# A decoder layer's gated MLP: the up product with the hi and lo parts of the activations side by side

## The chip, the cores and the metric

One core of one Trainium2 chip runs the whole program. The metric is the device time of one execution in microseconds, as the median of several executions.

## The reference

One layer of a decoder on 256 tokens of width 1024, in float32. The change lies in the second half, the gated MLP with a causal convolution of width 3, which is all that is quoted here:

```python
x = x + merged.astype(x.dtype) @ w_out[i]
x = x + conv_ffn(rmsnorm(x, norm_ffn[i]), w_up[i], conv_w[i], conv_b[i], w_down[i])
return rmsnorm(x, norm_final)

def rmsnorm(x, g):
    y = xf * lax.rsqrt(jnp.mean(xf * xf, axis=-1, keepdims=True) + RMS_EPS)
    return y * g

def conv_ffn(x, w_up, conv_w, conv_b, w_down):
    h = x @ w_up                        # (256, 1024) @ (1024, 5632)
    h = depthwise_causal_conv3(h, conv_w) + conv_b
    a, u = jnp.split(h, 2, axis=-1)     # 2816 columns each
    return (jax.nn.silu(a) * u) @ w_down
```

## The kernel before

**Numbers in two parts.** Each float32 operand of a product is split into a rounded part, hi, and the rest, lo, both of type fp32r. A product is three matmuls: lo times hi, hi times lo, hi times hi. The helper `mm3` (L238) issues them, at L239, L240 and L241, so nearly all of TensorE's rows carry one of these three lines. In `mm3` the second argument pair is the stationary side (loaded by LDWEIGHTS), the third the moving side.

**Weights.** They come from memory in units of 128 x 2048 elements (class `Unit`): one DMA on SP's queue into `raw` (L218), then in two halves of 1024 columns ScalarE copies the hi part (L223, `whi`) and VectorE subtracts for the lo part (L227, `wlo`). Five buffers of each kind rotate. The MLP uses per step i (0 to 10) the units `fa{i}`, `fu{i}` (up weights of the a and u columns) and `fd{i}` (down weights).

**The up product.** Tokens are on the moving side: `h_hi` and `h_lo` (tiles `hn_hi`, `hn_lo`) hold the activations transposed, 8 tiles of 128 rows (k) by 256 tokens, times the norm's weight but not yet divided by the norm's root. For each chunk ch of 128 columns (22 of a, 22 of u), `up` (L891) makes 8 times `mm3`, so 24 matmuls of 256 columns, into one of four PSUM tiles `g`. `by_rstd` (L792, L795) then multiplies by the row factor `rows` on VectorE, into one of three quarters of tile `xn1`; this also frees the PSUM tile.

**The rest of a chunk.** `conv` is one ScalarE activation (L879) and two VectorE operations (L881) in tile `cy`; SiLU of a is on ScalarE (L899), the gate product on VectorE (L901, `sa`), then the split into `fh` (ScalarE, L904) and `fl` (VectorE, L905). `later` (L702) queues the down product of the chunk: 12 matmuls of 512 columns into the four sums `acc`, issued one chunk later (three later for the last three chunks). The first of these 12 has `fl` on its stationary side, so TensorE waits there if `fl` is late.

**The way into the MLP.** Up to L867 the order on the engines is written by hand: the residual add, squares, the transposes of x into the four `acc` banks (`turned`, list `xT`), the split into `h_hi`, `h_lo` (`turn_hi` L786 on ScalarE, `turn_lo` L789 on VectorE), the products of chunk 0 and 1 of both sides (`firsts`), and `rows` (L851). From L869 on the order within each engine is the scheduler's; each engine runs its list strictly in that order.

Of the kernel before, what the change touches and what calls it, by code (L numbers as in the profile page):

```python
# [10 lines left out]
F32 = mybir.dt.float32  # L11
F32R = mybir.dt.float32r
# [3 lines left out]

P = 128
WARM = 16
S = 256
D = 1024  # L20
KC = D // P
# [106 lines left out]
def decoder_layer(ctx: ExitStack, tc, x, small_b, table, w1, wts, norms, out):  # L128
# [112 lines left out]
        nc.tensor.matmul(ps, ah, bh, start=False, stop=stop)  # L241

    mix = ctx.enter_context(tc.tile_pool(name="mix", bufs=1))
    o_hi = mix.tile([P, KC, S], F32R, name="o_hi")
    o_lo = mix.tile([P, KC, S], F32R, name="o_lo")
    mixer = ctx.enter_context(ExitStack())
    qkv = mixer.enter_context(tc.tile_pool(name="qkv", bufs=1))
    att = mixer.enter_context(tc.tile_pool(name="att", bufs=1))
# [433 lines left out]
    turn = [0]  # L682

    def gtile():
        turn[0] ^= 1
        return pools[turn[0]].tile([P, 512], F32, name="g")[:, :S]

    late = ctx.enter_context(tc.tile_pool(name="late", bufs=1))

# [73 lines left out]
    h_hi, h_lo = normed_tiles()  # L763
    spare = [act_pool.tile([P, D], F32, name=f"xn{t}") for t in range(NT)]
    rows, scaled = spare[1][:, 0:S], [spare[1][:, i * S:(i + 1) * S] for i in range(1, 4)]
    HALF = [slice(n * 512, (n + 1) * 512) for n in range(2)]

    def add(t, n):
# [23 lines left out]
    def by_rstd(ps):  # L792
        u = scaled.pop(0)
        scaled.append(u)
        nc.vector.tensor_mul(u, ps, rows)  # L795
        return u

    fu = dict(first)
    firsts = [gtile() for _ in range(4)]
# [9 lines left out]
    with tc.manual_schedule(engines={mybir.EngineType.Activation, mybir.EngineType.DVE, mybir.EngineType.Pool,  # L809
                                     mybir.EngineType.PE}):  # L810

        sq = {}
        for t in range(NT):
            flush(t, 0)
            add(t, 0)
            sq[t, 0] = square(t, 0)
        flush(0, 1)
        add(0, 1)
        xT += turned(0)
        flush(1, 1)  # L820

        def split_x(c0):

            for c in (c0, c0 + 1):
                turn_hi(c)
            for c in (c0, c0 + 1):
                turn_lo(c)
        split_x(0)
        add(1, 1)
        split_x(2)  # L830
        for t in range(NT):
            sq[t, 1] = square(t, 1)
        first_products(0, h_hi, range(4))

        rs = [rstd_of([sq[t, 0], sq[t, 1]], f"f{t}") for t in range(NT)]
        xT += turned(1)
        first_products(0, h_lo, range(4))
        split_x(4)
        split_x(6)
        for i in range(2):  # L840
            u_f.lo(i, 2)
        u_n = Unit("fa1")
        fu["fa1"] = u_n.views
        for i in range(2):
            u_n.hi(i, 2)
        first_products(0, h_hi, range(4, KC))

        rp = psa.tile([P, 512], F32, name="acc00")[:, :S]
        for t in range(NT):
            nc.tensor.matmul(rp[:, t * P:(t + 1) * P], rs[t].to_broadcast([P, P]), ident, start=True, stop=True)  # L850
        on_act = [nc.scalar.activation(rows, rp, AF.Copy)]  # L851
        for i in range(2):
            u_n.lo(i, 2)
        first_products(0, h_lo, range(4, KC))
        u_n = Unit("fu1")
        fu["fu1"] = u_n.views
        for i in range(2):
            u_n.hi(i, 2)
        for i in range(4):
            for k in range(KC):  # L860
                u = fu[("fa0", "fu0")[i % 2]]
                nc.tensor.matmul(firsts[i], u[1][:, k, i // 2 * P:(i // 2 + 1) * P], h_hi[:, k, :], start=False,  # L862
                                 stop=k == KC - 1)
            if i < 3:
                firsts[i] = by_rstd(firsts[i])
            if i < 2:
                on_dve = u_n.lo(i, 2)  # L867
    waiting.clear()
    with tc.issue_after(on_act[0].ins), tc.issue_after(on_dve.ins):  # L869
        fu["fd0"] = unit("fd0")  # L870


    merge.close()
# [11 lines left out]
    for i in range(NFF // 2):  # L885
        with tc.issue_after(on_act[3 + i].ins) if i in (1, 2) else ExitStack():
            ua, uu, ud = [fu.pop(f"f{w}{i}", None) or unit(f"f{w}{i}") for w in "aud"]
        for c in range(2):
            ch = 2 * i + c

            def up(u):  # L891
                ps = gtile()
                for k in range(KC):
                    mm3(ps, u[0][:, k, c * P:(c + 1) * P], u[1][:, k, c * P:(c + 1) * P],
                        h_hi[:, k, :], h_lo[:, k, :], k == 0, k == KC - 1)
                return by_rstd(ps)
            a = conv(firsts[2 * ch] if ch < 2 else up(ua), ch)
            sa = mpool.tile([P, S], F32, name="sa")
            nc.scalar.activation(sa, a, AF.Silu)  # L899
            b = conv(firsts[1] if ch == 0 else by_rstd(firsts[3]) if ch == 1 else up(uu), NFF + ch)  # L900
            nc.vector.tensor_mul(sa, sa, b)  # L901
            fh = mpool.tile([P, S], F32R, name="fh", bufs=4)
            fl = mpool.tile([P, S], F32R, name="fl", bufs=4)
            nc.scalar.activation(fh, sa, AF.Copy)  # L904
            nc.vector.tensor_sub(fl, sa, fh.bitcast(F32))  # L905
            later(acc, fh, fl, ud, c, ch == 0, ch == NFF - 1, 1 if ch < NFF - 3 else 3)
# [39 lines left out]
```

## Time and profile before

| | us |
|---|---|
| median of three executions | 432.51 |
| the three | 432.37, 432.51, 433.72 |
| the profiled execution | 432.46 |
| its span, first to last instruction | 430.7 |
| TensorE busy in the span | 420.8 |
| VectorE busy | 307.1 |
| ScalarE busy | 240.0 |

The span starts at the first instruction and all stamps count from there. Busy matmuls overlap in the profile, so their pace is read from the distance of their starts, not from their durations. A group "x4" is a run of four operations with their joint duration.

### The profile page before, as it was taken

Reading aid. Unit: us, or ns where it says so; the run is one execution under the profiler, and the core shown is the slowest. Engines: PE = TensorE matmul, PEld = TensorE weight load, DVE = VectorE, ACT = ScalarE, POOL = GpSimd, SP = SyncE. Lnnn points to the kernel's source line nnn. Section 1 sums busy time; section 2 is a strip of 40 time slices with the busy share of each in tenths; the row PEclk is TensorE's granted clock in tenths of the full one; section 3 lists DMA queues with packets and bytes.
Section 4 is the critical chain, followed back from the end, with each engine's and each line's share of the span. In section 5 each row is a group of like instructions: output and inputs, shape, how many; then the busy total and the mean of one; then the engine's idle time right before and its main releaser. Section 6 shows DMA issues by size and latency. Waiting matters only on the chain.

```text
span 430.7 us, 7724 instructions
## 1 busy us (share of the span) xinstructions
PE 420.8 (98%) x3104; PEld 388.3 (90%) x3104; DVE 307.1 (71%) x637; ACT 240.0 (56%) x421; POOL 12.9 (3%) x19
## 2 busy tenths in 40 slices
PE   8999999999999999999999999999999999999993
PEld 8998888887789998999998999999999999999982
DVE  4756753798874697539255899888697797786854
ACT  6443282448777774454346868457465465574423
POOL 3301000000000000000000000000000000000001
PEclk9999999999999999999999999999999999999998
DMA  8989619431209784554530367673462652700002
GB/s 299 397 321 326 238 68 367 177 130 75 99 5 339 288 327 168 196 189 158 189 151 0 139 253 257 231 269 135 183 256 81 251 203 95 290 0 2 2 0 97
DMA packets 12611, 78.09 MB, mean 181 GB/s; under 512 B 1392, under 2 KB 1408, under 8 KB 4640
## 3 DMA queue, kind: packets, MB, share of 16 engines
q1 hardware_dynamic: 12000, 75.48, 46.8%
q0 software_dynamic: 576, 2.12, 1.5%
q8 instruction: 24, 0.39, 0.4%
q14 instruction: 11, 0.09, 0.1%
HBM read 76.52 MB, written 1.07 MB: 180 GB/s over the span
## 4 chain that ended last, share of the span: by engine, by line
PE 90%; ACT 3%; issue 2%; DMA 2%; DVE 1%; POOL 1%; POOLq 0%; SPq 0%; ACTq 0%
PE g L239 21%; PE g L241 20%; PE g L240 20%; PE acc L239 6%; PE acc L240 6%; PE acc L241 6%; PE o L488 2%; PE t L469 2%; PE g L806 2%; DMA raw<-in_wts_dram 2%; PE s L455 1%; PE g L862 1%; PE o L555 1%; ACT tt L506 1%; POOL wlo L227 1%
## 5 line engine op out<-in xcount | busy, mean ns | idle before, releaser
L227 DVE TENSOR_TENSOR wlo<-raw,whi 128x1024 fp32r<-128x1024 f32 (+2 forms) x130 | 152.7, 1205 | 47.6 <-ACT whi L223 47.3
L239 PE MATMUL g<-hn_hi,wlo 128*128 128x256 f32 x632 | 180.4, 285 | 0.1
L240 PE MATMUL g<-hn_lo,whi 128*128 128x256 f32 x632 | 180.0, 285 | 0.0
L241 PE MATMUL g<-hn_hi,whi 128*128 128x256 f32 x632 | 179.7, 284 | 0.0
L223 ACT ACTIVATE whi<-raw 128x1024 fp32r<-128x1024 f32 (+2 forms) x130 | 129.2, 1038 | 37.7 <-PE g L241 30.6
L239 PEld LDWEIGHTS g<-hn_hi,wlo 128*128 128x128 f32 x632 | 121.1, 192 | 3.4 <-issue 1.4
L240 PEld LDWEIGHTS g<-hn_lo,whi 128*128 128x128 f32 x632 | 121.1, 192 | 1.2 <-issue 0.5
L241 PEld LDWEIGHTS g<-hn_hi,whi 128*128 128x128 f32 x632 | 121.2, 192 | 1.0 <-issue 1.0
L881 DVE SCALAR_TENSOR_TENSOR cy<-xn,small_b,cy 128x255 f32<-128x255 f32 (+1 forms) x88 | 41.7, 481 | 10.8 <-ACT cy L879 9.8
L879 ACT ACTIVATE cy<-xn,small_b 128x256 f32<-128x256 f32 x44 | 26.1, 594 | 17.2 <-DVE xn L795 17.2
L239 PE MATMUL acc<-whi,fl 128*128 128x512 f32 x88 | 34.6, 393 | 0.0
L240 PE MATMUL acc<-wlo,fh 128*128 128x512 f32 x88 | 34.4, 391 | 0.0
L241 PE MATMUL acc<-whi,fh 128*128 128x512 f32 x88 | 34.2, 389 | 0.0
L904 ACT ACTIVATE fh<-sa 128x256 fp32r<-128x256 f32 x22 | 9.1, 414 | 33.1 <-DVE sa L901 33.1
L795 DVE TENSOR_TENSOR xn<-g,xn 128x256 f32<-128x256 f32 x44 | 18.5, 421 | 9.6 <-PE g L241 9.0
L673 ACT ACTIVATE gl<-g 128x256 f32<-128x256 f32 x24 | 9.1, 378 | 21.7 <-PE g L241 21.7
L241 PEld LDWEIGHTS acc<-whi,fh 128*128 128x128 f32 x88 | 16.5, 188 | 3.6
L239 PEld LDWEIGHTS acc<-whi,fl 128*128 128x128 f32 x88 | 16.6, 188 | 3.1
L240 PEld LDWEIGHTS acc<-wlo,fh 128*128 128x128 f32 x88 | 16.6, 189 | 2.8
L239 PE MATMUL g<-o_hi,wlo 128*128 128x256 f32 x64 | 18.2, 286 | 0.0
L240 PE MATMUL g<-o_lo,whi 128*128 128x256 f32 x64 | 18.1, 283 | 0.0
L241 PE MATMUL g<-o_hi,whi 128*128 128x256 f32 x64 | 17.9, 283 | 0.0
(180 smaller groups left out, 495.6 us busy)
## 6 DMA issues: line engine op xcount, KB each, us to landing
raw<-in_wts_dram SPq DMA_DIRECT2D x62, 1024.0 KB, 4.9
gl<-in_w_dram SPq DMA_DIRECT2D x8, 512.0 KB, 7.4
raw<-in_wts_dram SPq DMA_DIRECT2D x2, 804.0 KB, 7.4
raw<-in_wts_dram SPq DMA_DIRECT2D x3, 512.0 KB, 7.1
T<-tvd POOLq DMA_DIRECT2D x1, 1280.0 KB, 12.9
xs<-in_x_dram SPq DMA_DIRECT2D x2, 516.0 KB, 3.7
out_dram<-raw SPq DMA_DIRECT2D x4, 256.0 KB, 2.2
T<-tvd POOLq DMA_DIRECT2D x1, 768.0 KB, 8.1
```

The lines of the kernel that those rows point to most:

```text
L223: nc.scalar.activation(self.parts[0][:, sl], self.raw[:, sl], AF.Copy)
L227: return (eng or nc.vector).tensor_sub(self.parts[1][:, sl], self.raw[:, sl], self.parts[0][:, sl].bitcast(F32))
L239: nc.tensor.matmul(ps, al, bh, start=start, stop=False)
L240: nc.tensor.matmul(ps, ah, bl, start=False, stop=False)
L241: nc.tensor.matmul(ps, ah, bh, start=False, stop=stop)
L469: nc.tensor.transpose(ps[:, i * P:(i + 1) * P], b, ident)
L488: nc.tensor.matmul(po[64 * h:64 * h + 64, cols], a, b, start=i == 0, stop=i == len(steps) - 1)
L673: nc.scalar.activation(gl[c][:, b, :], chunk_T(plain(u, c)), AF.Copy)
L795: nc.vector.tensor_mul(u, ps, rows)
L879: on_act.append(nc.scalar.activation(y, u, AF.Identity, bias=vec_c[:, 3, ch:ch + 1], scale=vec_c[:, 2, ch:ch + 1]))
L881: nc.vector.scalar_tensor_tensor(y[:, sh:], u[:, :S - sh], vec_c[:, w, ch:ch + 1], y[:, sh:], op0=ALU.mult, op1=ALU.add)
L904: nc.scalar.activation(fh, sa, AF.Copy)
```

## The change

From step i = 3 on (`NORMED = 3`, so 16 chunks of a and 16 of u), the up product reads the activations from one new tile `parts` (`h_parts`), in which for every k the hi and the lo part of the normed activations stand side by side: 512 columns. The two matmuls that have the weights' hi part on the stationary side, times `h_hi` and times `h_lo`, become one of 512 columns over both halves; the one with the weights' lo part stays, 256 columns. So a chunk has 16 matmuls in place of 24. The right half of the PSUM bank holds hi times lo and has to be added: ScalarE copies it to SBUF (tile `xn0`), and VectorE adds it to the left half, where `by_rstd` stood. Since no factor is applied there any more, the activations in `parts` are already divided by the root: `weighted_T` (ScalarE, 8 operations of 128 x 256) writes x times the norm's weight into two tiles `gl`, and `norm_parts`, called twice when i = 2, multiplies by `rows` (VectorE, 128 x 1024), copies the hi part (ScalarE, 128 x 1024) and subtracts for the lo part (VectorE, 128 x 1024). Chunks 0 to 5 keep the old way, with `h_hi`, `h_lo` and `by_rstd`. `o_hi` and `o_lo` of the attention part become halves of one tile of the same name `parts`, whose place is used again here.

```diff
+NORMED = 3
-    o_hi = mix.tile([P, KC, S], F32R, name="o_hi")
-    o_lo = mix.tile([P, KC, S], F32R, name="o_lo")
+    o_parts = mix.tile([P, KC, 2, S], F32R, name="parts")
+    o_hi, o_lo = o_parts[:, :, 0, :], o_parts[:, :, 1, :]
...
+    copies = [spare[0][:, i * S:(i + 1) * S] for i in range(4)]
...
+    h_parts = mix.tile([P, KC, 2, S], F32R, name="parts")
+    whole = [mix.tile([P, 4, S], F32, name="gl", bufs=4) for _ in range(2)]
+
+    def weighted_T(c):
+        nc.scalar.activation(whole[c // 4][:, c % 4, :], xT[c], AF.Copy, scale=g_ffn[:, c:c + 1])
+
+    def norm_parts(i):
+        sl = slice(4 * i, 4 * i + 4)
+        nc.vector.tensor_mul(whole[i], whole[i], rows[:, None, :].to_broadcast([P, 4, S]))
+        nc.scalar.activation(h_parts[:, sl, 0, :], whole[i], AF.Copy)
+        nc.vector.tensor_sub(h_parts[:, sl, 1, :], whole[i], h_parts[:, sl, 0, :].bitcast(F32))
...
             sq[t, 1] = square(t, 1)
+        for c in range(2):
+            weighted_T(c)
         first_products(0, h_hi, range(4))
...
         fu["fd0"] = unit("fd0")
+        for c in range(2, KC):
+            weighted_T(c)
...
+        if i == NORMED - 1:
+            for part in range(2):
+                norm_parts(part)
...
             def up(u):
-                ps = gtile()
+                cols = slice(c * P, (c + 1) * P)
+                ps = bank()
+                if i < NORMED:
+                    for k in range(KC):
+                        mm3(ps[:, :S], u[0][:, k, cols], u[1][:, k, cols], h_hi[:, k, :], h_lo[:, k, :], k == 0, k == KC - 1)
+                    return by_rstd(ps[:, :S])
                 for k in range(KC):
-                    mm3(ps, u[0][:, k, c * P:(c + 1) * P], u[1][:, k, c * P:(c + 1) * P],
-                        h_hi[:, k, :], h_lo[:, k, :], k == 0, k == KC - 1)
-                return by_rstd(ps)
+                    hi = lambda: nc.tensor.matmul(ps, u[0][:, k, cols], h_parts[:, k].rearrange("p a q -> p (a q)"),
+                                                  start=k == 0, stop=k == KC - 1)
+                    lo = lambda: nc.tensor.matmul(ps[:, :S], u[1][:, k, cols], h_parts[:, k, 0, :], start=False, stop=False)
+                    for product in ((lo, hi) if k else (hi, lo)):
+                        product()
+                v, part = scaled.pop(0), copies.pop(0)
+                scaled.append(v)
+                copies.append(part)
+                nc.scalar.activation(part, ps[:, S:], AF.Copy)
+                nc.vector.tensor_add(v, ps[:, :S], part)
+                return v
```

What it does to the order on the engines is shown at three places. Line numbers of the changed kernel are its own: `mm3` stands at L240 to L242, the new matmuls at L924 and L926.

On TensorE, in one up product of the later steps: before, three matmuls of 256 columns for each k.

```order
L239 MATMUL g_3810<-hn_hi_2803,wlo_3788 128x256
L240 MATMUL g_3810<-hn_lo_2804,whi_3787 128x256
L241 MATMUL g_3810<-hn_hi_2803,whi_3787 128x256
L239 MATMUL g_3810<-hn_hi_2803,wlo_3788 128x256
L240 MATMUL g_3810<-hn_lo_2804,whi_3787 128x256
L241 MATMUL g_3810<-hn_hi_2803,whi_3787 128x256
```

In the changed kernel, the same place of another chunk (L924 has the weights' hi part, L926 their lo part):

```order
L924 MATMUL g_3770<-parts_2806,whi_3747 128x512
L926 MATMUL g_3770<-parts_2806,wlo_3748 128x256 x2
L924 MATMUL g_3770<-parts_2806,whi_3747 128x512
L926 MATMUL g_3770<-parts_2806,wlo_3748 128x256
L924 MATMUL g_3770<-parts_2806,whi_3747 128x512
```

Two matmuls stand for three, in turn; the weights change with each matmul as before.

On VectorE, where the first down product is prepared (the tile `fl` of chunk 0); before:

```order
L901 TENSOR_TENSOR sa_3035<-sa_3035,cy_3037 128x256
L795 TENSOR_TENSOR xn1_2806<-g_3114,xn1_2806 128x256
L881 SCALAR_TENSOR_TENSOR cy_3053<-xn1_2806,small_b_377,cy_3053 128x255
L905 TENSOR_TENSOR fl_3043<-sa_3035,fh_3042 128x256
L881 SCALAR_TENSOR_TENSOR cy_3053<-xn1_2806,small_b_377,cy_3053 128x254
L901 TENSOR_TENSOR sa_3050<-sa_3050,cy_3053 128x256
L227 TENSOR_TENSOR wlo_3076<-raw_3074,whi_3075 128x1024
L905 TENSOR_TENSOR fl_3059<-sa_3050,fh_3058 128x256
```

and in the changed kernel (L939 and L943 are the old L901 and L905, L903 the old L881, L228 the old L227, L800 the old L795):

```order
L939 TENSOR_TENSOR sa_3045<-sa_3045,cy_3047 128x256
L800 TENSOR_TENSOR xn1_2805<-g_3124,xn1_2805 128x256
L812 TENSOR_TENSOR gl_2807<-gl_2807,xn1_2805 128x1024
L943 TENSOR_TENSOR fl_3053<-sa_3045,fh_3052 128x256
L903 SCALAR_TENSOR_TENSOR cy_3063<-xn1_2805,small_b_376,cy_3063 128x255
L228 TENSOR_TENSOR wlo_3086<-raw_3084,whi_3085 128x1024
L903 SCALAR_TENSOR_TENSOR cy_3063<-xn1_2805,small_b_376,cy_3063 128x254
L228 TENSOR_TENSOR wlo_3086<-raw_3084,whi_3085 128x1024
L939 TENSOR_TENSOR sa_3060<-sa_3060,cy_3063 128x256
```

The first multiplication of `norm_parts` (L812) has moved in ahead of the first `fl`, and the second `fl` stands five operations later. On TensorE the scheduler has put the first down products apart: before, those of chunk 0 and 1 follow each other after 64 up matmuls; now chunk 0's come after 70, and chunk 1's 15 up matmuls later.

On VectorE, further on, where the other three operations of `norm_parts` stand in the changed kernel (behind `fl` of chunk 3):

```order
L943 TENSOR_TENSOR fl_3235<-sa_3201,fh_3234 128x256
L814 TENSOR_TENSOR parts_2806<-gl_2807,parts_2806 128x4x256
L812 TENSOR_TENSOR gl_2808<-gl_2808,xn1_2805 128x1024
L800 TENSOR_TENSOR xn1_2805<-g_3280,xn1_2805 128x256
L800 TENSOR_TENSOR xn1_2805<-g_3312,xn1_2805 128x256
L228 TENSOR_TENSOR wlo_3440<-raw_3438,whi_3439 128x1024
L814 TENSOR_TENSOR parts_2806<-gl_2808,parts_2806 128x4x256
```

The second L814 is the last operation that the first new up product needs; the conversion of the weights of step 3 (L228, unit `fa3`) stands between them.

## Rows read from the trace of the kernel before

**Rows 1.** The chain that ended last, shares of the span by engine.
```profile
PE 90%; ACT 3%; issue 2%; DMA 2%; DVE 1%; POOL 1%; POOLq 0%; SPq 0%; ACTq 0%
```

**Rows 2.** Who made TensorE wait, whole span: total us, times, longest.
```profile
PE g L288 <- POOL tt L259: 1.0, 1, 1.0
...
PE g L356 <- POOL wlo L227: 0.2, 1, 0.2
```

**Rows 3.** Stretches: us, PE, PEld, DVE, ACT, POOL busy, granted clock, DMA share, GB/s.
```profile
244.00:262.00 18.00, 18.00 (x129) 16.90 (x129) 17.34 (x32) 13.07 (x20) 0.00 (x0) 1.00 0.70 267
262.00:283.00 21.00, 21.00 (x152) 19.84 (x151) 19.44 (x32) 14.20 (x21) 0.00 (x0) 1.00 0.66 240
283.00:405.00 122.00, 122.00 (x871) 115.29 (x870) 98.67 (x160) 68.13 (x101) 0.00 (x0) 1.00 0.41 152
```

**Rows 4.** Timeline of TensorE, last up product and flush: start, us, what.
```profile
409.62 0.28 PE L239 MATMUL g<-hn_hi,wlo 128*128 128x256 f32 x1
...
412.38 0.28 PE L241 MATMUL g<-hn_hi,whi 128*128 128x256 f32 x1
412.50 0.40 PE L239 MATMUL acc<-whi,fl 128*128 128x512 f32 x1
...
416.60 0.39 PE L239 MATMUL acc<-whi,fl 128*128 128x512 f32 x1
...
417.28 0.39 PE L239 MATMUL acc<-whi,fl 128*128 128x512 f32 x1
```

**Rows 5.** Timeline of TensorE, a change from 512 to 256 columns.
```profile
310.00 0.39 PE L241 MATMUL acc<-whi,fh 128*128 128x512 f32 x1
310.22 0.28 PE L239 MATMUL g<-hn_hi,wlo 128*128 128x256 f32 x1
310.34 0.28 PE L240 MATMUL g<-hn_lo,whi 128*128 128x256 f32 x1
```

**Rows 6.** Timeline of ScalarE on the way into the MLP, with idle before.
```profile
237.53 1.57 ACT L786 ACTIVATE hn_hi<-acc,xs 128x256 fp32r<-128x256 f32 x4 [0.84 <-PE acc L779]
...
242.24 0.38 ACT L851 ACTIVATE xn<-acc 128x256 f32<-128x256 f32 x1 [1.25 <-PE acc L850]
242.52 3.90 ACT L223 ACTIVATE whi<-raw 128x1024 fp32r<-128x1024 f32 x4
246.31 0.59 ACT L879 ACTIVATE cy<-xn,small_b 128x256 f32<-128x256 f32 x1
...
248.58 0.60 ACT L879 ACTIVATE cy<-xn,small_b 128x256 f32<-128x256 f32 x1 [0.86 <-DVE xn L795]
```

**Rows 7.** Timeline of VectorE around the first two `fl`.
```profile
250.73 2.06 DVE L881 SCALAR_TENSOR_TENSOR cy<-xn,small_b,cy 128x255 f32<-128x255 f32 x5
...
254.16 0.42 DVE L795 TENSOR_TENSOR xn<-g,xn 128x256 f32<-128x256 f32 x1
254.62 0.48 DVE L881 SCALAR_TENSOR_TENSOR cy<-xn,small_b,cy 128x255 f32<-128x255 f32 x1
255.02 0.42 DVE L905 TENSOR_TENSOR fl<-sa,fh 128x256 fp32r<-128x256 f32 x1
...
256.21 1.22 DVE L227 TENSOR_TENSOR wlo<-raw,whi 128x1024 fp32r<-128x1024 f32 x1
257.34 0.42 DVE L905 TENSOR_TENSOR fl<-sa,fh 128x256 fp32r<-128x256 f32 x1
257.68 1.22 DVE L227 TENSOR_TENSOR wlo<-raw,whi 128x1024 fp32r<-128x1024 f32 x1
```

**Rows 8.** Timeline of all engines: the first matmul of the first down product.
```profile
255.59 0.47 PE L239 MATMUL acc<-whi,fl 128*128 128x512 f32 x1
```

**Rows 9.** Timeline of VectorE: the last chunk's u product, and its `fl`.
```profile
412.70 0.42 DVE L795 TENSOR_TENSOR xn<-g,xn 128x256 f32<-128x256 f32 x1 [0.78 <-PE g L241]
...
415.74 0.43 DVE L905 TENSOR_TENSOR fl<-sa,fh 128x256 fp32r<-128x256 f32 x1 [0.49 <-ACT fh L904]
```

**Rows 10.** Timeline of ScalarE: the convolution's start behind it.
```profile
413.16 0.60 ACT L879 ACTIVATE cy<-xn,small_b 128x256 f32<-128x256 f32 x1 [0.73 <-DVE xn L795]
```

More of the change, by code (lines that the diff above doesn't have):

```diff
@@ L684, in gtile, with bank @@
     def gtile():
+        return bank()[:, :S]
+    def bank():
         turn[0] ^= 1
-        return pools[turn[0]].tile([P, 512], F32, name="g")[:, :S]
+        return pools[turn[0]].tile([P, 512], F32, name="g")
     late = ctx.enter_context(tc.tile_pool(name="late", bufs=1))
```

## The prediction

> **What bounds the kernel now.** I read the chain of work that ended last first: TensorE carries 90% of the span [rows 1]. Then the list of what TensorE waited for: five rows, all with a count of one, the longest 1.0 us and the shortest 0.2 us, on lines of the norm at the start and of the attention; none on a line of the MLP [rows 2]. The table by stretches says the same: from 244 to 405 us TensorE is busy all the time at a granted clock of 1.00, which is the level of 2.4 GHz [rows 3]. So in the MLP the time is the sum of the distances at which matmuls start, and a change is worth what it takes from that sum, minus the waits it brings. The same table shows the danger: VectorE is busy for 17.34 of 18.00 us from 244 to 262 and for 19.44 of 21.00 from 262 to 283, while from 283 to 405 it is 98.67 of 122.00.
>
> The distances: from 409.62 to 412.38 there are 23 steps of 256-column matmuls, 2.76 us, so 0.1200 us each; from 412.50 to 417.28 there are 21 steps of 512-column ones, 4.78 us, so 0.2276 each [rows 4]. Twice 0.1200 is 0.2400: a 512-column matmul is 0.0124 us cheaper than two of 256. The difference of the two steps, 0.1076, is the price of 256 columns, so each matmul with its own weight load carries 0.0124 us beyond its columns. That is what the change can save, once for each pair that it joins.
>
> **The change part by part.**
>
> *The joined matmuls.* The order shows 16 matmuls in place of 24 in each up product from step 3 on. For each k there stood 3 x 0.1200 = 0.3600 us; now 0.2276 + 0.1200 = 0.3476. With 8 k and 16 + 16 products this is 256 x 0.0124 = 3.17 us. Wide and narrow matmuls alternate now, which the trace of before shows only at the change of groups: after a wide one at 310.00 the next starts 0.22 later, and the one after that 0.12 later [rows 5]. So neither step grows by the neighbour, and I take the full 3.17. As bounds: nothing, if each half of the wide one paid again; 4.0 us as the upper end, an estimate of a quarter more, for narrow steps that shrink a little beside a wide one, which no row shows.
>
> The Trainium skill, "TensorE: Matmul & The Clock Gate", section "Back-to-back issue gap", gives the warm gap as the columns over 2.4 GHz plus 2.5 ns. By it a joined pair saves 2.5 ns, and the sum would be 256 x 2.5 ns = 0.64 us (an estimate by that page). The same rows differ from it: what a matmul carries here beyond its columns is 12.4 ns.
>
> *ScalarE's copy and VectorE's add.* The add has the shape of the multiplication it replaces, 0.42 us [rows 9], so VectorE's load stays. ScalarE gets 32 copies of 128 x 256 out of PSUM at 0.38, the row of `rows` [rows 6], together 12.2 us; it is busy 68.13 of 122.00 us from 283 to 405 [rows 3], so it has 53.87 free. In the middle of the MLP a chunk's result is used only after two further up products, 2 x 2.78 us, so 0.4 us more on its way is covered. A PSUM tile stays taken 0.4 us longer, with four tiles of 2.78 us each: covered too.
>
> *The tail.* At the end the cover is thin. The last `fl` starts at 415.74 and takes 0.43, so it ends at 416.17; TensorE uses it at 416.60, the nineteenth matmul of the flush [rows 4, 9]. The slack is 0.43. The copy adds 0.38 and a handoff of 0.04 (VectorE's 412.70 + 0.42 = 413.12 to ScalarE's 413.16 [rows 9, 10]): 0.42. TensorE reads the weights side a little ahead, so I take a wait of 0.1 to 0.25 us: 0.2. If nothing hid it, 0.42.
>
> *The eight weighted copies on ScalarE.* Two stand in the hand-written order ahead of the copies that begin at 237.53, after an idle time of 0.84 [rows 6]. Four operations of the same kind took 1.57, so 0.39 each; two are 0.78, which fits. The other six, 2.35 us, stand behind the conversion that ends at about 246.4 and ahead of the three convolution starts. These begin at 246.31 to 248.58 now [rows 6]; pushed back to 248.66 and following each other at 0.5, the third ends at about 250.25. VectorE takes the first at 250.73 [rows 7]. Hidden, with 0.5 to spare; without that cover at most 2.35 us.
>
> *The normalising on VectorE.* Four operations of 128 x 1024 come in, each 1.13 us of VectorE's time (256.21 to 257.34 [rows 7]): 4.52 us in the crowded stretch; ScalarE's two 1024-column copies fit its idle time. In rows 3 VectorE has 0.66 + 1.56 = 2.22 us free there, so it must live on what it had done early. Whether TensorE notices is read at the first matmul of each down product, which needs `fl`. I counted forward along the changed order from VectorE's operation at 254.16, with 1.13 for 1024 columns, 0.40 for a convolution step (254.62 to 255.02) and 0.34 for the others of 256 columns (257.34 to 257.68) [rows 7], adding 0.42 for `fl` itself; and on TensorE from 255.59 [rows 8] plus six narrow steps, 256.31, with the steps above:
>
> - chunk 0: `fl` done 256.05, TensorE there at 256.31
> - chunk 1: 260.59 against 260.84
> - chunk 2: 265.07 against 265.37
> - chunk 3: 271.81 against 273.38
> - chunk 4: 281.89 against 282.34
> - chunk 5: 290.50 against 291.21
>
> So it fits at every place, with 0.25 us as the smallest slack. That is close: any handoff of a third of a microsecond that I have not counted is seen. The second operation L814, last before the first new product, falls at about 277; TensorE needs `parts` at 281.9. I take no wait, and keep 0 to 1.5 us for the range.
>
> *Weights.* The order of the loads is the same. A raw buffer comes free when VectorE has subtracted from it, which in the crowded stretch is later by at most the 4.52 us of new work; the DMA engines are at a share of 0.66 to 0.70 there and of 0.41 behind it [rows 3], so a late load catches up. I take nothing; a load that came too late would cost at most those 4.52 us, the price of the third rival.
>
> **Sum.** 3.17 - 0.2 = 2.97, say 3.0 us. The profiled execution took 432.46 us with a span of 430.7, the median is 432.51; the span should become 427.7, and the time 432.51 - 3.0 = 429.5 us, 0.7% less.
>
> **The rivals.**
>
> *Waits at the seams eat a good part.* Slacks of 0.25, 0.26 and 0.30 are used up by uncounted handoffs, and each delay is handed to the next `fl`, since VectorE has no gap until chunk 3. For it: VectorE's 17.34 of 18.00. Against it: my count uses full durations and the scheduler has moved TensorE's groups apart to the same end. Price: 1 to 2.5 us of waits, so 430.5 to 432.0; the middle, 431.2, lies at the border of what counts as no change.
>
> *The pair saves only a bare gap.* If what a matmul carries comes from its columns and weight side in a way that the joining does not touch, one pair saves a small part of the 12.4 ns; with a fifth of it, 0.64 - 0.2 = 0.4 us and 432.1. Against it: wide matmuls that load their weights each time do run at 0.2276 [rows 4]. The page above would have it so.
>
> *Slower: VectorE becomes the bound between 254 and 283.* If the four operations come on top of a list that TensorE already follows without slack, TensorE waits for all of it, 4.52 us, and 4.52 - 3.0 makes it 1.5 us slower: 434.0. For it: rows 3. Against it: the count above has all four operations in it and still finds a slack at each place. It decides from total waits of 3.0 us on; beyond 4.3 it can be measured.
>
> *That it does not do what it says:* the order shows the joined matmuls and the same weight DMAs, so I give this no chance of its own.
>
> **How the numbers follow.** A measurement of this kernel tells some 0.3% (1.3 us) from no change: faster means below 431.2, slower above 433.8. My forecast 0.70 (428.9 to 430.5), waits at the seams 0.15 (half below 431.2, half above), the bare gap 0.08, VectorE as the bound 0.07. Faster: 0.70 + 0.08 = 0.78; same: 0.07 + 0.08 = 0.15; slower 0.07. The range runs from 428.6, the upper end of the saving (432.51 - 4.0, with no tail), to 432.0, the worse end of the seams; the bare gap and the slower case, 0.15, are left out.
>
> **What would show it.** Right: starts in the new up products alternate by 0.228 and 0.120 us, eight pairs in 2.78; no row of waits of TensorE on `fl` above 0.3 us between 255 and 292; the end of TensorE's chain moves by 3 us while the 13.4 us from the flush's matmul at 417.28 to the span's end stay. Wrong in the first step: pairs at 0.35 to 0.36. Wrong in the normalising: TensorE idle before `acc` at L240 between 256 and 283, released by VectorE. Wrong in the tail: an idle time over 0.4 us at the nineteenth matmul of the flush.

## The result and the profile after

The changed kernel takes 430.12 us (median of six executions, 429.01 to 430.74), the kernel before beside it 432.54 (432.23 to 433.72): a ratio of 0.994, with an interval of 0.9929 to 0.9952. That is a gain of 2.4 us where 3.0 were forecast. A second measurement of the same kernel gave 3.0 us (experiment 1). The profiled execution was the fastest of the six: 429.01 us, with a span of 427.2.

The head of the changed kernel's page, with busy time, share of the span and number of instructions of each engine, and the shares of the chain that ended last, the answer to [rows 1]:

```profile
PE 417.7 (98%) x2848; PEld 373.8 (87%) x2848; DVE 309.6 (72%) x641; ACT 253.6 (59%) x463; POOL 13.1 (3%) x19
...
PE 89%; ACT 4%; DVE 4%; issue 2%; POOL 0%; POOLq 0%; ACTq 0%
```

TensorE still carries the chain. ScalarE gained 13.6 us of work (240.0 before) and VectorE 2.5 (307.1). The list of what made TensorE wait (total us, times, longest) has four rows now, all on lines of the norm at the start and of the attention. The longest stands here; it is the wait that heads [rows 2] too:

```profile
PE g L289 <- POOL tt L260: 1.0, 1, 1.0
```

No row on a line of the MLP came in. The table by stretches, columns as in [rows 3], with the last end moved by the 3 us gained:

```profile
244.00:262.00 18.00, 18.00 (x133) 17.17 (x132) 17.61 (x32) 15.99 (x28) 0.00 (x0) 1.00 0.70 262
262.00:283.00 21.00, 21.00 (x145) 19.56 (x145) 20.86 (x34) 15.27 (x21) 0.00 (x0) 1.00 0.57 208
283.00:402.00 119.00, 119.00 (x634) 102.08 (x633) 98.69 (x161) 75.45 (x130) 0.00 (x0) 1.00 0.43 160
```

The last stretch is 119 us instead of 122, its VectorE work is the same to 0.02 us, and its matmuls are 634 instead of 871. VectorE is now busy for 20.86 of 21.00 us from 262 to 283, and TensorE beside it still for all 21.00.

**Where the 3.46 us of the span went.** The spans are 430.69 and 427.23. I cut both executions at the same four matmuls: the first of all, the first of the MLP's early products with the weights' lo part (`firsts`; called MLP below), the first of the flush (the 48 down matmuls that are left behind the last up product), and the last (us, from start to start):

| kernel | first to MLP | MLP to flush | flush | behind the last |
|---|---|---|---|---|
| before | 242.96 | 168.54 | 10.68 | 7.51 |
| after | 242.16 | 165.56 | 11.01 | 7.50 |

So the MLP gained 2.98, the flush lost 0.33, and 0.80 lie ahead of the MLP, where the change has only put two operations on ScalarE and the order on the engines is otherwise the same. That stretch took between 242.16 and 243.76 in the profiles of the changed kernel and of the eight runs below (242.55 when the very same kernel ran again), so I count the 0.80 as the luck of this execution. What the change itself does is 2.98 - 0.33 = 2.65 us.

**A product.** Timeline of TensorE in the changed kernel: start, duration, line and operands; a chunk's first down matmul (331.02), its a product (from 333.75) and u product, and the next chunk's first down matmul (339.34):

```profile
331.02 0.39 PE L240 MATMUL acc<-whi,fl 128*128 128x512 f32 x1
...
333.75 0.39 PE L924 MATMUL g<-parts,whi 128*128 128x512 f32 x1
...
334.56 0.40 PE L924 MATMUL g<-parts,whi 128*128 128x512 f32 x1
...
335.98 0.40 PE L924 MATMUL g<-parts,whi 128*128 128x512 f32 x1
...
337.38 0.39 PE L924 MATMUL g<-parts,whi 128*128 128x512 f32 x1
...
338.76 0.39 PE L924 MATMUL g<-parts,whi 128*128 128x512 f32 x1
...
339.34 0.39 PE L240 MATMUL acc<-whi,fl 128*128 128x512 f32 x1
```

Two products take 339.34 - 333.75 = 5.59 us, so 2.795 each; the forecast was 2.78 and before it was 2.88 (unrounded 2.873 for an a product, right behind down matmuls, and 2.880 for the others). In the a product four pairs take 335.98 - 334.56 = 1.42 us, 0.355 each; in the u product 338.76 - 337.38 = 1.38, 0.345 each. From the unrounded starts a whole a product takes 2.813 (0.352 a pair) and a whole u product 2.777 (0.347), in every chunk of this form. A chunk, from `acc` to `acc`, takes 8.31 us (339.339 - 331.025 unrounded).

The kernel before, same view, from one chunk's first down matmul to the next:

```profile
307.36 0.28 PE L241 MATMUL g<-hn_hi,whi 128*128 128x256 f32 x1
307.48 0.40 PE L239 MATMUL acc<-whi,fl 128*128 128x512 f32 x1
...
308.87 0.39 PE L239 MATMUL acc<-whi,fl 128*128 128x512 f32 x1
...
315.98 0.40 PE L239 MATMUL acc<-whi,fl 128*128 128x512 f32 x1
```

315.98 - 307.48 = 8.50 a chunk. These rows hold what the forecast passed over: behind the narrow matmul at 307.36 the first six wide ones take 308.87 - 307.48 = 1.39, 0.231 each, and the other six up to 310.22 [rows 5] take 1.36 by the unrounded starts, 0.2265 each. A wide matmul is slower for a while after narrow ones, and in the changed kernel every wide one but a product's first stands behind a narrow one. There the unrounded wide steps are 231 to 241 ns and the narrow ones 112 to 120. In a u product the two make up for each other: 16 steps at the settled 0.120 and 0.2267 would take 2.773, and it takes 2.777. The a product, at 2.813, pays 0.04.

**The tail.** TensorE in the changed kernel, from the flush's first matmul (behind the last u product) through the nineteenth matmul of the flush, which answers to [rows 4]:

```profile
408.72 0.39 PE L240 MATMUL acc<-whi,fl 128*128 128x512 f32 x1
...
412.58 0.39 PE L242 MATMUL acc<-whi,fh 128*128 128x512 f32 x1
413.02 0.50 PE L240 MATMUL acc<-whi,fl 128*128 128x512 f32 x1
413.36 0.40 PE L241 MATMUL acc<-wlo,fh 128*128 128x512 f32 x1
```

ScalarE and VectorE there, where the added copy (L932) and add (L933) stand, with the idle time before and its releaser (L937 is the SiLU of a):

```profile
408.77 0.42 ACT L937 ACTIVATE sa<-cy 128x256 f32<-128x256 f32 x1 [1.13 <-DVE cy L903]
409.10 0.37 ACT L932 ACTIVATE xn<-g 128x256 f32<-128x256 f32 x1
...
409.50 0.42 DVE L933 TENSOR_TENSOR xn<-g,xn 128x256 f32<-128x256 f32 x1 [0.82 <-ACT xn L932]
...
412.55 0.42 DVE L943 TENSOR_TENSOR fl<-sa,fh 128x256 fp32r<-128x256 f32 x1 [0.48 <-ACT fh L942]
```

The last `fl` ends at 412.97, TensorE takes it at 413.02; the matmul before started at 412.58. The step is 0.44 instead of 0.227, and the next, 413.02 to 413.36, is 0.34: a wait of 0.22 and 0.11 more until the pace is back, the 0.33 of the table. From the flush's first matmul to the end of the last `fl` it is 412.97 - 408.72 = 4.25 now; before it was 416.17 - 412.50 = 3.67 [rows 4, 9]. Of these 0.58, 0.40 lie between the starts of copy and add. The other 0.18 lie ahead of the copy: it starts 0.38 behind the flush's first matmul, where the multiplication that it precedes started 0.20 behind it before. ScalarE is then still in the SiLU (408.77 to 409.19), which stands ahead of the copy in its order.

### The profile page after: what moved, and what is told of

It reads as the page before. It is cut to its first block, busy times and chain, and to the rows that moved or that the text cites. A ratio compares the mean times of both kernels' runs of the same rounds, so it can differ in the third digit from the quotient of the medians.

```text
span 427.2 us, 7237 instructions
## 1 busy us (share of the span) xinstructions
PE 417.7 (98%) x2848; PEld 373.8 (87%) x2848; DVE 309.6 (72%) x641; ACT 253.6 (59%) x463; POOL 13.1 (3%) x19
## 4 chain that ended last, share of the span: by engine, by line
PE 89%; ACT 4%; DVE 4%; issue 2%; POOL 0%; POOLq 0%; ACTq 0%
PE g L240 14%; PE g L242 13%; PE g L241 13%; PE g L924 12%; PE g L926 6%; PE acc L240 6%; PE acc L241 6%; PE acc L242 6%; PE o L489 2%; PE t L470 2%; PE g L824 2%; PE g L289 1%; PE s L456 1%; DVE cy L903 1%; PE g L882 1%
## 5 line engine op out<-in xcount | busy, mean ns | idle before, releaser
L228 DVE TENSOR_TENSOR wlo<-raw,whi 128x1024 fp32r<-128x1024 f32 (+2 forms) x130 | 153.9, 1204 | 48.4 <-ACT whi L224 47.7
L240 PE MATMUL g<-hn_hi,wlo 128*128 128x256 f32 x376 | 108.2, 288 | 0.1
L241 PE MATMUL g<-hn_lo,whi 128*128 128x256 f32 x376 | 107.5, 286 | 0.0
L242 PE MATMUL g<-hn_hi,whi 128*128 128x256 f32 x376 | 107.2, 285 | 0.0
L924 PE MATMUL g<-parts,whi 128*128 128x512 f32 x256 | 89.4, 396 | 0.0
L240 PEld LDWEIGHTS g<-hn_hi,wlo 128*128 128x128 f32 x376 | 72.0, 191 | 2.9 <-issue 1.4
L242 PEld LDWEIGHTS g<-hn_hi,whi 128*128 128x128 f32 x376 | 72.0, 192 | 1.1 <-issue 1.0
L241 PEld LDWEIGHTS g<-hn_lo,whi 128*128 128x128 f32 x376 | 72.0, 192 | 0.7 <-issue 0.5
L926 PE MATMUL g<-parts,wlo 128*128 128x256 f32 x256 | 66.2, 279 | 0.0
L924 PEld LDWEIGHTS g<-parts,whi 128*128 128x128 f32 x256 | 46.7, 188 | 9.2
L926 PEld LDWEIGHTS g<-parts,wlo 128*128 128x128 f32 x256 | 48.2, 188 | 2.8
L903 DVE SCALAR_TENSOR_TENSOR cy<-xn,small_b,cy 128x255 f32<-128x255 f32 (+1 forms) x88 | 41.4, 478 | 8.9 <-ACT cy L901 8.0
L240 PE MATMUL acc<-whi,fl 128*128 128x512 f32 x88 | 34.5, 392 | 0.1
L242 PE MATMUL acc<-whi,fh 128*128 128x512 f32 x88 | 34.2, 389 | 0.0
L901 ACT ACTIVATE cy<-xn,small_b 128x256 f32<-128x256 f32 x44 | 25.8, 598 | 7.4 <-DVE xn L933 7.4
L932 ACT ACTIVATE xn<-g 128x256 f32<-128x256 f32 x32 | 12.2, 380 | 22.2 <-PE g L924 22.2
L242 PEld LDWEIGHTS acc<-whi,fh 128*128 128x128 f32 x88 | 16.5, 188 | 3.6
L933 DVE TENSOR_TENSOR xn<-g,xn 128x256 f32<-128x256 f32 x32 | 13.4, 420 | 8.4 <-ACT xn L932 8.4
```

The lines of the kernel that those rows point to most:

```text
L228: return (eng or nc.vector).tensor_sub(self.parts[1][:, sl], self.raw[:, sl], self.parts[0][:, sl].bitcast(F32))
L240: nc.tensor.matmul(ps, al, bh, start=start, stop=False)
L241: nc.tensor.matmul(ps, ah, bl, start=False, stop=False)
L901: on_act.append(nc.scalar.activation(y, u, AF.Identity, bias=vec_c[:, 3, ch:ch + 1], scale=vec_c[:, 2, ch:ch + 1]))
L903: nc.vector.scalar_tensor_tensor(y[:, sh:], u[:, :S - sh], vec_c[:, w, ch:ch + 1], y[:, sh:], op0=ALU.mult, op1=ALU.add)
L924: hi = lambda: nc.tensor.matmul(ps, u[0][:, k, cols], h_parts[:, k].rearrange("p a q -> p (a q)"), start=k == 0, stop=k == KC - 1)
```

## The experiments

All were timed in five rounds beside the kernel before on the same chip: experiments 1 to 4 on one (before 432.47, 23 executions), 5 to 8 on another (432.63, 17 executions). "MLP to flush" and "flush" are the columns of the table above, from each one's profile.

| | median (range) us | ratio to before | MLP to flush | flush |
|---|---|---|---|---|
| 1 again | 429.48 (429.31–429.9) | 0.9926 [0.9912, 0.9940] | 165.57 | 11.04 |
| 2 split | 431.61 (430.83–432.36) | 0.9976 [0.9966, 0.9987] | 167.45 | 11.09 |
| 3 tail old | 429.25 (428.77–430.3) | 0.9921 [0.9905, 0.9937] | 165.67 | 10.67 |
| 4 normed 2 | 432.71 (431.27–434.68) | 1.0007 [0.9989, 1.0024] | 169.31 | 11.05 |
| 5 from 7 | 430.66 (430.42–431.84) | 0.9954 [0.9939, 0.9969] | 167.00 | 11.00 |
| 6 norm only | 432.33 (431.64–433.46) | 0.9999 [0.9988, 1.0010] | 168.43 | 10.68 |
| 7 grouped | 429.24 (429.12–430.44) | 0.9924 [0.9909, 0.9938] | 165.43 | 11.01 |
| 8 wide first, tail old | 429.96 (428.78–430.2) | 0.9930 [0.9915, 0.9946] | 165.49 | 10.67 |

My theory: the gain is what a matmul carries beyond its columns, saved once for each joined pair, minus the tail. The rivals: the gain comes from the new order or from the normalising (and the pair saves only a bare gap); and what is missing to 3.0 us is lost in waits at the seams.

**1. The changed kernel again.** No edit.

> The changed kernel once more, as the partner of the other runs on this chip. Theory (each joined pair saves what a matmul carries beyond its columns, 12.4 ns, less a wait of 0.2 us in the flush): 2.4 to 3.0 us below the kernel before, with the distance from the first products with the weights' lo part to the first matmul of the flush near 165.6 us (168.5 before). If the early lead of 0.8 us that the profile of the changed kernel showed ahead of the MLP was chance, it is not there in this profile.

The gain is 2.99 us here, and 2.42 in the first measurement. MLP to flush agrees to 0.01 us between the two profiles (165.56 and 165.57), while the stretch ahead of it is 242.16 in one and 242.55 in the other. So the times scatter with what lies ahead of the MLP, and the segment is the finer scale for the rest.

**2. The wide matmul as two narrow ones**, for six of the eight k, with all else as in the changed kernel.

```
 def hi():
+    for a in ((slice(0, 2),) if k in (0, KC - 1) else (slice(0, 1), slice(1, 2))):
+        nc.tensor.matmul(ps[:, a.start * S:a.stop * S], u[0][:, k, cols],
+                         h_parts[:, k, a].rearrange("p a q -> p (a q)"), start=k == 0, stop=k == KC - 1)
-    nc.tensor.matmul(ps, u[0][:, k, cols], h_parts[:, k].rearrange("p a q -> p (a q)"), ...)
```

> The changed kernel, but for 6 of the 8 k the 512-column matmul is issued as two of 256 columns into the two halves (192 pairs split again; copy, add and normalising stay). Theory of the saved matmul: 192 x 0.0124 = 2.4 us slower than the changed kernel, about 432.5, level with the kernel before. Rival, a bare gap of 2.5 ns for each pair: 0.5 us slower than the changed kernel, 430.6. Rival, the rest of the change has a cost of its own at the seams: clearly above the kernel before, 433 or more.

MLP to flush rises by 167.45 - 165.57 = 1.88 us for 6 x 32 = 192 pairs: 9.8 ns a pair. The medians differ by 2.13. TensorE in this kernel, four k of a product (L926 twice is the split wide one, L928 the narrow one with the weights' lo part):

```profile
330.16 0.40 PE L926 MATMUL g<-parts,whi 128*128 128x256 f32 x2
330.40 0.28 PE L928 MATMUL g<-parts,wlo 128*128 128x256 f32 x1
...
331.59 0.40 PE L926 MATMUL g<-parts,whi 128*128 128x256 f32 x2
```

Four k take 1.43 us, 0.358 each, against 0.345 to 0.355 when joined. The joining is the gain; the expected 2.4 us was too high, since it took the forecast's 12.4 ns. The bare-gap rival gave 0.5 us and falls, and so does a cost at the seams, which would have shown 433 or more. A joined pair does away with one matmul and with one weight load (this kernel has 192 more of each than the changed one); which of the two carries the time beyond the columns no run separates.

The Trainium skill, "TensorE: Matmul & The Clock Gate", section "Back-to-back issue gap", has 2.5 ns beyond the columns for an isolated matmul at the higher clock, by which these 192 pairs would be worth 0.5 us (an estimate by that page). The trace disagrees, with 9.8 ns a pair.

**3. The last u product the old way** (three narrow matmuls, no copy).

```
-def up(u):
+def up(u, old=False):
...
-    if i < NORMED:
+    if i < NORMED or old:
...
-... else up(uu), NFF + ch)
+... else up(uu, ch == NFF - 1), NFF + ch)
```

> The changed kernel, but the very last up product (the u side of chunk 21) goes the old way, with 24 narrow matmuls and no copy on ScalarE. Theory of the thin cover in the tail: the wait ahead of the nineteenth matmul of the flush goes (0.22 us, and the slow restart behind it, 0.1), the product itself takes 0.1 longer: 0.1 to 0.3 us less than the changed kernel, about 429.9. Rival, that wait is no matter of the copy: 0.1 us more than the changed kernel and the gap of 0.45 us still there.

TensorE in this kernel, at the eighteenth and nineteenth matmul of the flush:

```profile
413.27 0.39 PE L242 MATMUL acc<-whi,fh 128*128 128x512 f32 x1
413.50 0.39 PE L240 MATMUL acc<-whi,fl 128*128 128x512 f32 x1
```

The step is 0.23, the gap is gone: the flush is 10.67 again, and the old product costs 0.10. MLP to the end of the flush is 176.34 instead of 176.61, so 0.27 us better in the trace; the two medians, 429.25 and 429.48, can't tell these 0.2 us from nothing. The joined form's longer way for the last chunk, over ScalarE's copy, is what the flush pays for.

**4. One step fewer on the old way**, so that the normed parts are needed two chunks earlier.

```
-NORMED = 3
+NORMED = 2
```

> The changed kernel with the joined form from step 2 on in place of step 3, so four more joined products and the normalising one step earlier, in the most crowded stretch of VectorE. Theory of the saved matmul alone: 4 x 0.085 = 0.34 us less than the changed kernel, 429.8. Rival, VectorE as the bound: the four operations come where it has no gap and the first joined product needs them about 14 us earlier, so TensorE waits there; a wait of over 0.4 us makes it slower than the changed kernel, 430.5 to 432.

As fast as the kernel before, by the median: the whole gain is gone. TensorE's waits on the MLP's lines in this kernel:

```profile
PE g L926 <- DVE wlo L228: 1.7, 1, 1.7
...
PE g L924 <- ACT whi L224: 0.4, 1, 0.4
```

VectorE there (timeline: start, duration, operation):

```profile
260.26 2.35 DVE L814 TENSOR_TENSOR parts<-gl,parts 128x1024 fp32r<-128x1024 f32 x2
...
266.82 1.22 DVE L228 TENSOR_TENSOR wlo<-raw,whi 128x1024 fp32r<-128x1024 f32 x1
```

The stretches of this kernel, with columns as in [rows 3]:

```profile
240.00:265.00 25.00, 25.00 (x189) 23.92 (x187) 24.33 (x38) 17.95 (x30) 0.00 (x0) 1.00 0.55 211
265.00:272.00 7.00, 4.92 (x17) 3.59 (x16) 7.00 (x14) 7.00 (x11) 0.00 (x0) 0.76 0.11 25
```

VectorE and ScalarE are busy for all 7.00 us from 265 to 272 and TensorE for 4.92: the third rival's mechanism, VectorE as the bound, one step of the program earlier. The new work has pushed back the split of the weights (`whi` of ScalarE, which ends the first wait below, and VectorE's `wlo`, ready at 268.04, which ends the second). Something came on top that no theory had. TensorE's timeline there, with the idle time before and its releaser:

```profile
265.63 0.73 PE L924 MATMUL g<-parts,whi 128*128 128x512 f32 x2 [0.36 <-ACT whi L224]
268.09 0.80 PE L926 MATMUL g<-parts,wlo 128*128 128x256 f32 x2 [1.72 <-DVE wlo L228]
268.69 0.63 PE L924 MATMUL g<-parts,whi 128*128 128x512 f32 x1
269.11 0.63 PE L240 MATMUL acc<-whi,fl 128*128 128x512 f32 x1
269.54 0.63 PE L241 MATMUL acc<-wlo,fh 128*128 128x512 f32 x1
...
271.21 0.40 PE L242 MATMUL acc<-whi,fh 128*128 128x512 f32 x1
```

After the two waits wide matmuls start 0.427 us apart (269.11 to 269.54) instead of 0.227, until about 271.2; the granted clock of the stretch is 0.76. That is the level of 1.2 GHz for a while. The price in this profile is 3.74 us against experiment 1, in spite of four joined products more: 2.08 of it is idle time, and the six wide steps from 268.69 to 271.21 took 2.52 instead of 1.37, 1.15 more. The rest lies in the slow steps around them: from the narrow matmul at 265.00 to 271.92, TensorE's starts take 6.92 us, where 3 narrow and 11 wide steps at 0.120 and 0.227 make 2.86. These 4.06 more, less 0.32 that four more joined products give back, are the 3.74. The twelve executions fall into two groups by their granted clock over the whole span: six at 0.995 to 0.997 took 431.27 to 432.53 (median 431.62), six at 0.992 to 0.993 took 432.90 to 434.68 (median 433.93). The first group is where the expectation put the waits (430.5 to 432); that its executions waited without losing the clock is inferred from these numbers, since the one profile is of the second group.

**5. Joined products only from step 7 on**: 16 instead of 32, with the normalising where it was.

```
-if i < NORMED:
+if i < 7:
```

> The changed kernel with the normalising where it is, but the joined form only from step 7 on: 16 joined products in place of 32. Theory of a fixed saving for each pair (2.88 us for an old product, 2.795 on average for a joined one in the trace of the changed kernel): half of the saving is gone, 16 x 0.085 = 1.4 us slower than the changed kernel; the distance from the first products with the weights' lo part to the flush grows from 165.6 to 166.9 us. Rival, the saving or a loss sits at the seams and not in the pairs: the time stays at that of the changed kernel within 0.3 us.

**6. No joined product at all, but all the normalising**, so that the parts are computed and never used.

```
-if i < NORMED:
+if i < 11:
```

> The changed kernel with all its normalising work (8 operations on ScalarE, 2 more there, 4 on VectorE) but no joined product: every chunk goes the old way, and the normalised tile is not used. Theory that the normalising is hidden: the same time as the kernel before within 0.3 us, the distance up to the flush 168.0 to 168.6. Rival, VectorE pays for the four operations at the seams: 169.5 or more there, 433.5 or more in all.

These two and experiment 1 make a dose line, with MLP to flush at 168.43 (none joined), 167.00 (16) and 165.57 (32): 1.43 us for each sixteen, 0.089 a product, 11 ns a pair. At zero the line meets the kernel before, 168.54, to 0.11 us, and the median of experiment 6 is that of before (ratio 0.9999). VectorE's and ScalarE's lists are the same here as in the changed kernel, operation for operation, from 230 to 284 us, with the normalising in them. So the 4.5 us of normalising on VectorE, the eight weighted copies and the changed order cost nothing, and the rival by which the order brings the gain falls.

The order gives the 0.11, though. TensorE in the kernel before, one matmul ahead of [rows 8]:

```profile
255.36 0.28 PE L239 MATMUL g<-hn_hi,wlo 128*128 128x256 f32 x1
```

and in the changed kernel, the last up matmul ahead of the first down matmul (255.39):

```profile
255.28 0.28 PE L240 MATMUL g<-hn_hi,wlo 128*128 128x256 f32 x1
```

Before, the step to the first down matmul (255.59) is 0.23 instead of 0.12: `fl` ended at 255.44 [rows 7], and TensorE waited 0.11 for it. In the changed kernel the step (255.275 to 255.393 unrounded) is 0.12, as in experiment 6. The list of waits doesn't show this wait, since the record of the matmul at 255.36 lasts until 255.64, past the start of the next.

The gap in the flush is absent in 6 and present in 5, as it should be when it hangs on the last product.

**7. Wide and narrow matmuls in runs**, to see whether the alternation is what makes a pair dearer than 0.3476: one wide, eight narrow, seven wide.

```
-for k in range(KC):
-    ...
-    for product in ((lo, hi) if k else (hi, lo)):
-        product()
+hi(0)
+for k in range(KC):
+    lo(k)
+for k in range(1, KC):
+    hi(k)
```

> The changed kernel with the joined product in another order: one wide matmul, then the eight narrow ones, then the seven wide ones, so that wide and narrow no longer alternate. If the alternation costs what the trace of the changed kernel shows beyond 0.1200 and 0.2276 (a product at 2.777 and 2.813 in turn in place of 2.781), each product takes 2.78: 0.45 us less over 32 products, 165.1 up to the flush. If the alternation is not the reason: 165.6 as before.

TensorE in this kernel (L923 wide, L925 narrow; one product from 333.93 to the second half of the run at 335.11):

```profile
333.93 0.39 PE L923 MATMUL g<-parts,whi 128*128 128x512 f32 x1
334.15 1.12 PE L925 MATMUL g<-parts,wlo 128*128 128x256 f32 x8
335.11 2.00 PE L923 MATMUL g<-parts,whi 128*128 128x512 f32 x8
```

From the unrounded starts the narrow steps are 113 ns for the one right behind the wide one and then 120; the wide steps behind the narrow run are 234, 235, 229, 232, 231, 227 and 226. The product comes to 2.793, MLP to flush to 165.43, against 2.795 and 165.57 for alternating ones. So alternation as such is not the price. One change from narrow to wide, which is felt for about five wide matmuls, costs a product 0.02 here, and seven of them cost 0.04 in an a product and nothing in a u product of the changed kernel, so rarer changes do not help much.

**8. Seven wide, eight narrow, one wide, and the last u product the old way**: the best order that I could think of, with the tail mended.

```
-for k in range(KC):
-    ...
+for k in range(KC - 1):
+    hi(k)
+for k in range(KC):
+    lo(k)
+hi(KC - 1)
```

> A try for a better version: seven wide matmuls, then the eight narrow ones, then the last wide one, and the very last up product the old way as in the third run. Expected: the flush without its gap (10.67 us), and with the same question as the run before it: 165.2 up to the flush if the alternation costs, 165.7 if not; in all 0.2 to 0.6 us less than the changed kernel.

TensorE in this kernel, an a and a u product (L923 wide, L925 narrow):

```profile
335.27 1.75 PE L923 MATMUL g<-parts,whi 128*128 128x512 f32 x7
336.86 1.11 PE L925 MATMUL g<-parts,wlo 128*128 128x256 f32 x8
337.81 2.00 PE L923 MATMUL g<-parts,whi 128*128 128x512 f32 x8
```

Behind the down matmuls, which are wide too, seven wide ones take 336.86 - 335.27 = 1.59, 0.227 each: no change of width, no price. The products are 2.772 and 2.793 in turn. MLP to the end of the flush is 176.16, the least of all and 0.45 below experiment 1. In the times nothing of this is seen (429.96 against 429.48 on the other chip; this profile needed 243.76 up to the MLP, the longest of all). What an order saves in the products it partly loses in the twelve down matmuls behind them (2.741 here, 2.720 in experiment 7, 2.724 in the changed kernel): a whole chunk takes 8.307 here, 8.307 in experiment 7 and 8.314 in the changed kernel. No version is faster than the changed kernel by an amount that these measurements show.

## Why the prediction was right, point by point

**The bound** was read rightly: TensorE's steps set the MLP's time, and what the change took from their sum came out of the MLP's part of the span one for one (the dose line, at 0.089 us a product). "None on a line of the MLP" was read from a list that hides short waits: the kernel before waited 0.11 us for its first `fl`.

**The joined matmuls: the term that was mis-sized.** The forecast had 0.0124 us a pair and 3.17 us in all. It measured 2.86 by the dose line. By the starts, the 32 products take 2.796 on average where they take 2.877 in experiment 6, 0.080 each and 2.57 in all; the 14 groups of twelve down matmuls that stand between them take 0.02 less each (2.727 instead of 2.747, as they now stand behind a wide matmul), 0.28 in all; together 2.85. The step that failed is "So neither step grows by the neighbour". It rested on a change from wide to narrow [rows 5], where the step behind does shrink (114 ns unrounded), and was applied to both directions. From narrow to wide the trace of before had the answer, ahead of those rows: 0.231 for the first six wide matmuls, 0.2265 for the last six. The mean wide step of [rows 4], 0.2276, mixes the two. Both steps move in the changed kernel, and the sum grows in the a products alone. By the forecast's own sign, "pairs at 0.35 to 0.36" means wrong: the a products' 0.352 falls just inside, the u products' 0.347 outside, on the number itself.

**The tail** was forecast at 0.2 and measured at 0.22 of wait, but the terms differ. The way is longer by 0.58, not 0.42, since the copy also stands behind the SiLU on ScalarE, which the forecast took to be free. Against the slack of 0.43 that leaves 0.15, and the matmul starts 0.05 behind the end of `fl`: 0.20. The forecast's allowance for reading the weights side ahead happened to have about the size of the queue that it left out. The restart at 0.34 instead of 0.227, another 0.11, was not in the sum either: 0.33 in all, between the forecast and its bound of 0.42.

**The weighted copies and the normalising** were hidden, as said; experiment 6 shows it by itself. The six copies stand where they were counted, the first two with no idle time behind them (ScalarE in the changed kernel; the conversion L791 ran at 237.53 behind an idle time of 0.84 before [rows 6]):

```profile
235.80 0.82 ACT L808 ACTIVATE gl<-acc,xs 128x256 f32<-128x256 f32 x2
236.73 1.57 ACT L791 ACTIVATE hn_hi<-acc,xs 128x256 fp32r<-128x256 f32 x4
...
245.51 2.29 ACT L808 ACTIVATE gl<-acc,xs 128x256 f32<-128x256 f32 x6
247.65 1.62 ACT L901 ACTIVATE cy<-xn,small_b 128x256 f32<-128x256 f32 x3
```

The third convolution start ends at 249.27 and VectorE takes the first at 249.93: 0.66 to spare where 0.5 was forecast. At the seams, first `fl` on VectorE for chunks 0, 1 and 3 of the changed kernel:

```profile
254.82 0.42 DVE L943 TENSOR_TENSOR fl<-sa,fh 128x256 fp32r<-128x256 f32 x1
...
259.34 0.41 DVE L943 TENSOR_TENSOR fl<-sa,fh 128x256 fp32r<-128x256 f32 x1
...
270.68 0.42 DVE L943 TENSOR_TENSOR fl<-sa,fh 128x256 fp32r<-128x256 f32 x1
```

The matmuls that need them, on TensorE:

```profile
255.39 0.46 PE L240 MATMUL acc<-whi,fl 128*128 128x512 f32 x1
...
260.00 0.40 PE L240 MATMUL acc<-whi,fl 128*128 128x512 f32 x1
...
272.56 0.40 PE L240 MATMUL acc<-whi,fl 128*128 128x512 f32 x1
```

| chunk | 0 | 1 | 2 | 3 | 4 | 5 |
|---|---|---|---|---|---|---|
| slack forecast | 0.26 | 0.25 | 0.30 | 1.57 | 0.45 | 0.71 |
| slack measured | 0.15 | 0.25 | 0.33 | 1.46 | 0.38 | 0.59 |

None turned into a late start; the step behind chunk 0's first down matmul is 0.30 instead of 0.23, in the kernel before (255.59 to 255.89) as in the changed one (255.39 to 255.69). Chunk 0's is short by 0.11 because the forecast counted TensorE from 255.59, a start that held the wait of 0.11. Counting forward along the order with durations of before gave every slack to 0.12 us, in a stretch where VectorE's free time (0.39 + 0.14 us measured, of 39) would have suggested a wait. The second L814 started at 275.09 and ended at 276.30, where about 277 was forecast; the first product that needs it starts at about 281.

**Weights**: the DMA share is 0.57 from 262 to 283, against 0.66, and no wait of TensorE on a load came in. The forecast's "nothing" holds in the changed kernel.

**The rivals.** Waits at the seams: none that the change brought. The bare gap: refuted by experiment 2 and the dose line. VectorE as the bound: not in this kernel, but real one step earlier (experiment 4), at a price of about 2 us without and 4 with the fall of the clock, by the medians of the two groups against experiment 1. So its chance was not idle; the margin that kept it away was the third step.

**The sum.** 2.86 for the pairs and 0.11 for the wait that went, less 0.33 for the tail, is 2.64; the segments say 2.65. The range's fast end has a slip: 432.51 - 4.0 is 428.5, not 428.6, and nothing hangs on it. The median, 430.12, lies 0.6 above the forecast of 429.5. The span came out at 427.2, half a microsecond under the forecast, but only because 0.80 us ahead of the MLP fell out in its favour. The stretch ahead varies by 1.6 us from profile to profile, over half of the whole effect.

## What to carry to other kernels

Where one engine is busy without a gap, price an edit by the distances of its starts in the sequence in which they will stand: read the step in both directions of every neighbour change, since a mean over a run mixes the first matmuls with the settled ones. Work that is moved to a nearly full engine can be free if it has somewhere to lie before its use; count the slack at each point where its results or those behind it are needed, and ask what one step earlier would do. At the end of a kernel nothing covers a longer chain, so keep the old way for the last piece: 0.27 us in the trace (experiment 3), though the times can't show it. Count there also what the new operation stands behind on its own engine.

## What the runs showed of the hardware

- Behind a run of narrow matmuls (256 columns) wide ones (512) take 229 to 236 ns from start to start and come back to 226 or 227 only after about five; a narrow one right behind a wide run takes 113 or 114 instead of 120 (the kernel before, experiment 7). Where the two alternate, wide ones take 231 to 241 and narrow ones 112 to 120 (the changed kernel). Why, these traces don't show.
- a and u products, made alike, differ reproducibly: 2.813 and 2.777 us, by 36 ns. The a product stands behind down matmuls, the u product behind an a product. That is not the reason: the last two a products of the changed kernel, right behind a u product, take 2.817. Not settled.
- Waits of 0.36 and 1.72 us close together were followed by about 2.5 us in which wide matmuls started 0.427 us apart, so waits can cost about twice their length (experiment 4: 2.08 us of idle time, 4.06 lost; seen in one profile, inferred for half of the executions from their clock).
- A wide matmul that starts behind a short wait is followed by one long step (0.34 instead of 0.227 us) before the pace is nearly back: in the flush of the changed kernel behind 0.22 us, and in experiment 4 behind 0.36.
